# Sums of products (Strassen-Winograd form) in a Hymba-style encoder: three PSUM banks for five, and wider dead products at the start

## The chip, the cores and the metric

The kernel runs on one core of one Trainium2 chip. The metric is the device time of one execution in microseconds (us), here the median of the runs shown. PE is TensorE (matmul), DVE VectorE, ACT ScalarE, POOL GpSimd, SP SyncE, which issues the DMAs.

## The reference

Two token streams (512 and 256 tokens, 768 in all, width 1024) go through two layers. Each layer is an attention block of three mixers with a residual, and then a SwiGLU FFN with a residual; only the FFN is touched by most of the change:

```
h = rms_norm(x, norm_ffn[l])
gate, up = split(h @ w_gate_up[l], 2)          # 1024 -> 2 x 2816
x = x + (silu(gate) * up) @ w_down[l]          # 2816 -> 1024
```

All is float32. The matmuls take operands split in a high and a low part (`fp32r`), so each product is three matmuls: high x high, high x low, low x high.

## The kernel before

**Plan.** The kernel does not issue instructions directly. Each piece of work is an operation of a `Plan` with a cost, a priority, the buffers it reads and writes, and one or more engines that may do it. The planner (`schedule`, `latest`, `emit`) lists all operations of the whole kernel in order, with modelled times, up to 16 times over, gives each buffer a place, picks the best of the orders, and only then issues each engine's instructions in it. So a change of cost or dependence anywhere may move work elsewhere. PSUM has 8 banks of 512 columns; buffers of kind `ANY` take any of them, kind `M` the last. A product that adds to a bank comes after every read of that bank that stands before it in the program.

**Start.** x is loaded in eight pieces, with the first weights between them. While they come, PE runs `WARM` dead matmuls on a tile of ones (line 543). Then the projections of the first head group run on the first 256 tokens, as weight splits (lines 592 and 593) and input splits (lines 650 to 653) come ready; line 834 (ACT, squares) is the first step behind them, and lines 877 and 885 the split and the transposes at the end of that chain.

**FFN, gate and up.** 22 blocks f of 128 gate and up columns; the first two in the plain way, the other 20 with seven products in place of eight (`PRODUCTS`, line 1140). The tokens are two halves of 384 and the input depth two halves of 512. The weights of a block are four 512-wide pieces, from which `sums` (line 1119) makes S1 to S4 in four DVE additions (line 1131), and then splits all seven in high (ACT, line 1134) and low (DVE or POOL, line 1135). `product` (line 1143) is one of the seven: 4 pieces of depth, 3 matmuls of 384 columns each, into one bank.

Before, the seven use five banks: X takes A11 A, then adds S2 T2, then adds S3 T3; Y takes A12 B, Z takes S4 D, W takes A22 T4, V takes S1 T1. After each product into X, ACT copies the bank (line 1193) to one of the four parts of an SBUF buffer `sg`; the other banks are added to parts by DVE (line 1198), five additions in all. Then all four parts are multiplied by the row of norm factors (line 1205), gate goes through Silu (line 1160), is multiplied by up (line 1161) and is written to a DRAM buffer, `spill`.

**FFN, down.** The 22 blocks are taken in five stretches: 6 plain, 4 with sums, 4 plain, 4 with sums, 4 plain. A stretch with sums (`seven`, line 1241) takes two pairs of blocks as depth (n = 2, so 6 matmuls for a product) and goes over 4 pairs of output columns c and c + 4. Its products are read from the banks by DVE, which adds them into x (line 1259): nine additions for a pair.

Of the kernel before, what the change touches and what calls it, by code (L numbers as in the profile page):

```python
# [8 lines left out]
F32 = mybir.dt.float32  # L9
F32R = mybir.dt.float32r  # L10
AF = mybir.ActivationFunctionType
OP = mybir.AluOpType
# [3 lines left out]
D = 1024  # L16
# [6 lines left out]
HALF = 384  # L23
# [4 lines left out]
FIRST_F = 2  # L28
EPS = 1e-6
NEG = -1e30  # L30
WARM = 26
NSTK = 1
RW = 127
GROUPS = ((0, 1), (2, 3, 4), (5, 6, 7))
# [337 lines left out]
def trunk(ctx: ExitStack, tc: tile.TileContext, t):  # L372
    nc = tc.nc
    ACT, DVE, POOL, PE, SP = nc.scalar, nc.vector, nc.gpsimd, nc.tensor, nc.sync
    P = Plan()
# [13 lines left out]
    X = sb("x", [KC, TOK])  # L389
    identr = sb("identr", [128], F32R)  # L390
    ident = identr.bitcast(F32)
    ones = sb("ones", [128], F32R)
# [23 lines left out]
    for i in range(2):  # L416
        at = [(16 + 5 * i + j) * TOK for j in range(5)]
# [71 lines left out]
    def act(n, fn, r=(), w=(), prio=0.0, sbuf=True, extra=0, after=()):  # L489
        return P.op("ACT", a_cost(n, sbuf, extra), fn, r, w, prio, after, lat=0.05)  # L490

    def dve(n, fn, r=(), w=(), prio=0.0, fast=False, lock=False, ptr=False):
        return P.op("DVE", v_cost(n, fast, ptr), fn, r, w, prio, lat=0.05, lock=lock)
# [42 lines left out]
    P.op("DVE", 0.2, lambda: DVE.memset(ones.bitcast(F32), 1.0), w=["ones"], prio=-100)  # L536
    act(128, lambda: ACT.copy(identr, tmp[0]), r=[tmp], w=["identr", "ident"], prio=-15)

    warm = P.buf("M")

    def warmup():
        for _ in range(WARM):
            PE.matmul(warm[0][:, 0:128], ones, ones, start=True, stop=True)

    P.op("PE", 4.0, warmup, r=["ones"], w=[warm], prio=-100)

    def load_gains(l, m, prio):
        b = P.buf("QKG")
# [570 lines left out]
    def sums(srcs, width, prio, after):  # L1119

        q = {m: P.buf("RX") for m in ("A11", "A22", "S1", "A12", "S3", "S2", "S4")}
        b = {m: P.buf("WG") for m in ("A11", "A12", "S2", "S4", "S3", "A22", "S1")}
        hi = lambda m: b[m][0][:, :width]
        lo = lambda m: b[m][0][:, 512:512 + width]
        raw = lambda m: q[m][0][:, :width]
        for m, i in (("A11", 0), ("S1", 2), ("A22", 3), ("A12", 1)):
            out = (lambda m=m: raw(m).rearrange("p (c d) -> p c d", c=srcs[i].shape[1])) if len(srcs[i].shape) == 3 else lambda m=m: raw(m)
            dma(128 * 4 * width, lambda out=out, i=i: SP.dma_start(out=out(), in_=srcs[i]), w=[q[m]], prio=prio, after=after)
        for out, x, y, op in (("S3", "S1", "A11", OP.subtract), ("S1", "S1", "A22", OP.add), ("S2", "A11", "S1", OP.subtract),
                              ("S4", "A12", "S2", OP.add)):  # L1130
            ew(width, lambda E, out=out, x=x, y=y, op=op: E.tensor_tensor(raw(out), raw(x), raw(y), op=op), r=[q[x], q[y]],  # L1131
               w=[q[out]], prio=prio, on="wadd")
        for m in b:
            act(width, lambda m=m: ACT.copy(hi(m), raw(m)), r=[q[m]], w=[(b[m], 0)], prio=prio)  # L1134
            ew(width, lambda E, m=m: E.tensor_tensor(lo(m), raw(m), hi(m).bitcast(F32), op=OP.subtract),  # L1135
               r=[q[m], (b[m], 0)], w=[(b[m], 1)], prio=prio, on="slo")
        return b


    PRODUCTS = (("A11", "A", "X"), ("A12", "B", "Y"), ("S2", "T2", "X"), ("S4", "D", "Z"), ("S3", "T3", "X"), ("A22", "T4", "W"),  # L1140
                ("S1", "T1", "V"))

    def product(wb, ub, bank, n, prio, tok, first, last, open_=True, at=0):
        for kk in range(0, n, 2):
# [10 lines left out]
    def emit_ffn(l, base, ends, row, U):  # L1155
# [24 lines left out]
        for f in range(FIRST_F, FC):  # L1180
            pr = base + f
            wb = sums([t["w_gu"][l, f, i] for i in range(4)], 512, pr - 1.5, ends)
            bank = {}
            sg = P.buf("SG")
            for x, (wn, un, bn) in enumerate(PRODUCTS):
                if bn not in bank:
                    bank[bn] = P.buf("ANY")
                pp = pr + 0.1 * x
                product(wb[wn], [U[k][un] for k in range(4)], bank[bn], 4, pp, utok, un == "A" or bn != "X", True)
                pw = pp - 0.05  # L1190
                if bn == "X":
                    i = ("A", "T2", "T3").index(un)
                    act(HALF, lambda sg=sg, i=i, b=bank["X"]: ACT.copy(sg[i], b[0][:, :HALF]), r=[bank["X"]], w=[(sg, i)],  # L1193
                        prio=pw, sbuf=False)
                else:
                    for dst, src, op in {"Y": ((0, 0, OP.add),), "Z": ((1, 1, OP.add),), "W": ((3, 2, OP.add),),
                                         "V": ((1, 1, OP.add), (2, 2, OP.add))}[bn]:
                        dve(HALF, lambda sg=sg, dst=dst, src=src, op=op, b=bank[bn]: DVE.tensor_tensor(  # L1198
                            sg[dst], sg[src], b[0][:, :HALF], op=op), r=[bank[bn], (sg, src)], w=[(sg, dst)], prio=pw)

            for h, (g, u) in enumerate(((0, 3), (1, 2))):
                rt = [(row, p) for p in ((2, 0) if h == 0 else (0, 1))]
                rv = lambda h=h: row[0][:, h * HALF:(h + 1) * HALF]
                for z, on in ((g, "rg"), (u, "ru")):
                    ew(HALF, lambda E, z=z, sg=sg, rv=rv: E.tensor_tensor(sg[z], sg[z], rv(), op=OP.mult), r=rt, w=[(sg, z)],
                       prio=pr + 0.5, on=on)
                lastsilu = gated(f, sg, g, u, h, pr + 0.5)
# [33 lines left out]
        def seven(f0, n, pd):  # L1241

            us = [operands(f0 + i, f0 + n + i, pd - 15 + 2 * i) for i in range(n)]
            parts = lambda b: [(b, 0), (b, 1)]
            m = 4 // n if n < 4 else 1
            for c2 in range(0, 4, m):
                src = lambda c, f: t["w_down"][l, c:c + m, :, f * 128:(f + n) * 128].rearrange("c p d -> p c d")
                wb = sums([src(c2, f0), src(c2, f0 + n), src(c2 + 4, f0), src(c2 + 4, f0 + n)], m * n * 128, pd + 2 * c2 - 3.5, ())
                for z in range(m):
                    c, bank = c2 + z, {}  # L1250
                    for x, (wn, un, bn) in enumerate(PRODUCTS):
                        if bn not in bank:
                            bank[bn] = P.buf("ANY")
                        pp = pd + 2 * c + 0.2 * x
                        product(wb[wn], [u[un] for u in us], bank[bn], n, pp, parts, un == "A" or bn != "X", True, at=z * n * 128)
                        for cc, h in {"A": ((c, 0),), "B": ((c, 0),), "T2": ((c, 1),), "D": ((c, 1),), "T3": ((c + 4, 0), (c + 4, 1)),
                                      "T4": ((c + 4, 0),), "T1": ((c, 1), (c + 4, 1))}[un]:
                            xv = lambda cc=cc, h=h: X[:, cc, h * HALF:(h + 1) * HALF]
                            dve(HALF, lambda xv=xv, b=bank[bn]: DVE.tensor_tensor(xv(), xv(), b[0][:, :HALF], op=OP.add), r=[bank[bn]],  # L1259
                                w=[("x", p, cc // 2) for p in ((2, 0) if h == 0 else (0, 1))], prio=pp - 2)  # L1260

        for ci, (n, sums_) in enumerate(DCH):
            pd = base + 100 + 20 * ci
# [169 lines left out]
```

## Time and profile before

| | |
|---|---|
| time, median of 3 runs | 1723.81 us (1723.49 to 1727.6) |
| the profiled execution: its time | 1724.8 us |
| its span, first to last instruction | 1722.9 us |
| PE, PE weight loads | 98%, 96% busy |
| DVE, ACT, POOL | 81%, 55%, 36% busy |

The profile is one execution. An engine's busy share is an average over stages; PE's busy time is modelled at its ends, since matmuls overlap. A line such as `PE ps L617 <- ACT y L1193: 2.6, 3, 1.4` says that PE stood 2.6 us in all, 3 times, 1.4 us the longest, until ACT's instruction of line 1193 had finished.

### The profile page before, as it was taken

The page shows a single profiled execution, that of the slowest core. Times are in us where ns is not written, and L with a number is a line of the kernel's source. Part 1 is how long each engine was busy: PE and PEld are TensorE (multiplying, and loading weights), DVE is VectorE, ACT ScalarE, POOL GpSimd, SP SyncE. Part 2 cuts the span into 40 slices and gives each one's busy share as a digit, 9 for nine tenths or more (in the row PEclk, how much of TensorE's full clock was granted, in tenths as well). Part 3 has the DMA queues.
Part 4 walks back from the last instruction along what each step waited for, and adds up shares of the span by engine and source line. Part 5 has one row for each costly group of instructions (what it writes and reads, how often), then busy time and mean ns, then how long its engine had stood idle before and what let it go on. Part 6 is the DMA issues. An engine that isn't in the chain of part 4 may idle for free. (4 is left out here: it accounts for less than half of the span.)

```text
span 1722.9 us, 31174 instructions
## 1 busy us (share of the span) xinstructions
PE 1687.9 (98%) x11434; PEld 1660.9 (96%) x11434; DVE 1390.4 (81%) x2609; ACT 943.7 (55%) x2194; POOL 614.1 (36%) x620
## 2 busy tenths in 40 slices
PE   9999999899999999999999999998999999999999
PEld 8999999899999999999999999997999999999999
DVE  7778678699988887778868886877999887868693
ACT  7877577574444444424458865866744444434230
POOL 1655254223433333224126633632242333323130
PEclk9999999999999999999999999999999999999999
DMA  6221111102433333524322201101133333334233
GB/s 182 73 69 39 38 47 40 50 31 89 132 99 103 97 103 112 155 57 130 97 64 65 77 25 38 57 26 50 47 126 101 102 101 102 108 116 138 80 111 99
DMA packets 102890, 145.31 MB, mean 84 GB/s; under 512 B 29008, under 2 KB 66896, under 8 KB 102736
## 3 DMA queue, kind: packets, MB, share of 16 engines
q1 hardware_dynamic: 102736, 143.31, 27.7%
q8 instruction: 90, 1.47, 0.4%
q14 instruction: 64, 0.52, 0.1%
HBM read 122.82 MB, written 20.45 MB: 83 GB/s over the span
## 5 line engine op out<-in xcount | busy, mean ns | idle before, releaser
L617 PE MATMUL ps<-u,w 128*128 128x384 f32 (+1 forms) x1588 | 526.8, 332 | 8.4 <-ACT y L1193 4.2
L618 PE MATMUL ps<-u,w 128*128 128x384 f32 (+1 forms) x1588 | 525.8, 331 | 0.0
L619 PE MATMUL ps<-u,w 128*128 128x384 f32 (+1 forms) x1588 | 525.6, 331 | 0.0
L617 PEld LDWEIGHTS ps<-u,w 128*128 128x128 f32 x1588 | 298.5, 188 | 11.9 <-ACT y L1193 6.4
L618 PEld LDWEIGHTS ps<-u,w 128*128 128x128 f32 x1588 | 298.5, 188 | 0.3 <-POOL u L1218 0.3
L619 PEld LDWEIGHTS ps<-u,w 128*128 128x128 f32 x1588 | 298.5, 188 | 0.0
L617 PE MATMUL ps<-w,u 128*128 128x256 f32 x768 | 227.1, 296 | 0.4 <-DVE ppa L835 0.2
L618 PE MATMUL ps<-w,u 128*128 128x256 f32 x768 | 219.4, 286 | 0.9 <-DVE w L593 0.7
L619 PE MATMUL ps<-w,u 128*128 128x256 f32 x768 | 219.2, 285 | 0.0
L618 PEld LDWEIGHTS ps<-w,u 128*128 128x128 f32 x768 | 148.6, 193 | 3.0 <-DVE w L593 2.0
L617 PEld LDWEIGHTS ps<-w,u 128*128 128x128 f32 x768 | 148.2, 193 | 2.1 <-DVE ppa L835 0.4
L592 ACT CAST w<-raw 128x1024 fp32r<-128x1024 f32 (+2 forms) x86 | 78.1, 908 | 129.6 <-PE ps L618 90.6
L619 PEld LDWEIGHTS ps<-w,u 128*128 128x128 f32 x768 | 148.4, 193 | 0.2
L1198 DVE TENSOR_TENSOR y<-y,ps 128x384 f32<-128x384 f32 x160 | 86.0, 548 | 59.9 <-PE ps L619 33.1
L617 PE MATMUL ps<-yt,w 128*128 128x256 f32 x392 | 114.1, 291 | 2.1 <-DVE x L1104 1.6
L1020 DVE TENSOR_TENSOR u<-ps,u 128x512 fp32r<-128x512 f32 (+1 forms) x160 | 98.2, 625 | 20.0 <-ACT u L1019 19.1
L618 PE MATMUL ps<-yt,w 128*128 128x256 f32 x392 | 111.8, 285 | 1.1 <-POOL yt L1090 0.8
L619 PE MATMUL ps<-yt,w 128*128 128x256 f32 x392 | 111.2, 284 | 0.0
L1034 PE MATMUL ps<-u 128*128 128x256 f32 (+1 forms) x592 | 102.9, 291 | 6.0 <-DVE u L1020 4.6
L619 PE MATMUL ps<-u,yt 128*128 128x384 f32 x292 | 97.5, 334 | 0.0
L617 PE MATMUL ps<-u,yt 128*128 128x384 f32 x292 | 97.5, 334 | 0.0
L618 PE MATMUL ps<-u,yt 128*128 128x384 f32 x292 | 97.5, 334 | 0.0
(284 smaller groups left out, 3972.3 us busy)
## 6 DMA issues: line engine op xcount, KB each, us to landing
spill<-y SPq DMA_DIRECT2D x86, 192.0 KB, 2.4
raw<-in_w_gu SPq DMA_DIRECT2D x63, 256.0 KB, 2.8
raw<-in_w_in SPq DMA_DIRECT2D x30, 512.0 KB, 3.7
p<-in_w_gu SPq DMA_DIRECT2D x44, 256.0 KB, 2.8
ppa<-in_w_gu SPq DMA_DIRECT2D x39, 256.0 KB, 2.9
raw<-in_w_out SPq DMA_DIRECT2D x16, 512.0 KB, 3.6
tbm<-in_w_gu SPq DMA_DIRECT2D x30, 256.0 KB, 2.9
raw<-in_w_down SPq DMA_DIRECT2D x16, 384.0 KB, 3.4
```

Of the source, the lines that this page charges most:

```text
L592: act(n, lambda raw=raw, hs=hs: ACT.copy(self.flat(0)[:, hs], raw[0][:, :n]), r=[raw], w=[(b, 0) + z], prio=pr)
L617: PE.matmul(out, a[0], b[0], start=start, stop=False, skip_group_check=on)
L618: PE.matmul(out, a[0], b[1], start=False, stop=False, skip_group_check=on)
L619: PE.matmul(out, a[1], b[0], start=False, stop=stop, skip_group_check=on)
L1020: dve(n, lambda n=n, pt=pt, ps_=ps_: DVE.tensor_tensor(ps_[1][:, :n], pt[0][:, :n], ps_[0][:, :n].bitcast(F32), op=OP.subtract), r=[pt, (p ...
L1034: PE.matmul(po[0][:, o:o + wd], v, ps_[i][:, z * wd:(z + 1) * wd], start=first and z == 0 and i == 0, stop=end and (last or more), **({} i ...
L1198: dve(HALF, lambda sg=sg, dst=dst, src=src, op=op, b=bank[bn]: DVE.tensor_tensor(sg[dst], sg[src], b[0][:, :HALF], op=op), r=[bank[bn], (s ...
```

## The change

Three things are changed together.

- The dead matmuls at the start are 15 of 512 columns in place of 26 of 128. They read a buffer `wide` of kind `YT`, which DVE fills with ones first.
- The seven products run in another order and in three banks. X takes A11 A, adds S2 T2, adds S3 T3, adds A22 T4; Y takes A12 B; V takes S1 T1 and adds S4 D. `OPENS` names the products that begin a bank. X is read after each of its four products and V after both of its two.
- What stands behind the products: in gate and up, ACT copies the bank after A, T2 and T1; DVE adds it after B, T3 and D; after T4, DVE multiplies the bank with the row and writes the fourth part, so the row product of that part is no more. In the down stretches each product is added into x once, seven additions for nine.

```diff
-WARM = 26
+WARM = 15
...
-    warm = P.buf("M")
+    warm, wide = P.buf("M"), P.buf("YT")
 
     def warmup():
         for _ in range(WARM):
-            PE.matmul(warm[0][:, 0:128], ones, ones, start=True, stop=True)
+            PE.matmul(warm[0], ones, wide[0], start=True, stop=True)
 
-    P.op("PE", 4.0, warmup, r=["ones"], w=[warm], prio=-100)
+    P.op("DVE", 0.35, lambda: DVE.memset(wide[0].bitcast(F32), 1.0), w=[wide], prio=-100)
+    P.op("PE", 4.0, warmup, r=["ones", wide], w=[warm], prio=-100)
...
-        b = {m: P.buf("WG") for m in ("A11", "A12", "S2", "S4", "S3", "A22", "S1")}
+        b = {m: P.buf("WG") for m in ("A11", "A12", "S2", "S1", "S3", "S4", "A22")}
...
-    PRODUCTS = (("A11", "A", "X"), ("A12", "B", "Y"), ("S2", "T2", "X"), ("S4", "D", "Z"), ("S3", "T3", "X"), ("A22", "T4", "W"),
-                ("S1", "T1", "V"))
+    PRODUCTS = (("A11", "A", "X"), ("A12", "B", "Y"), ("S2", "T2", "X"), ("S1", "T1", "V"), ("S3", "T3", "X"), ("S4", "D", "V"),
+                ("A22", "T4", "X"))
+    OPENS = ("A", "B", "T1")
...
-                product(wb[wn], [U[k][un] for k in range(4)], bank[bn], 4, pp, utok, un == "A" or bn != "X", True)
-                pw = pp - 0.05
-                if bn == "X":
-                    i = ("A", "T2", "T3").index(un)
-                    act(HALF, lambda sg=sg, i=i, b=bank["X"]: ACT.copy(sg[i], b[0][:, :HALF]), r=[bank["X"]], w=[(sg, i)],
-                        prio=pw, sbuf=False)
+                product(wb[wn], [U[k][un] for k in range(4)], bank[bn], 4, pp, utok, un in OPENS, True)
+                pw, at, z = pp - 0.05, lambda b=bank[bn]: b[0][:, :HALF], {"A": 0, "B": 0, "T2": 1, "T1": 2, "T3": 2, "D": 1, "T4": 3}[un]
+                if un in ("A", "T2", "T1"):
+                    act(HALF, lambda sg=sg, z=z, at=at: ACT.copy(sg[z], at()), r=[bank[bn]], w=[(sg, z)], prio=pw, sbuf=False)
+                elif un == "T4":
+                    dve(HALF, lambda sg=sg, z=z, at=at: DVE.tensor_tensor(sg[z], at(), row[0][:, :HALF], op=OP.mult),
+                        r=[bank[bn], (row, 2), (row, 0)], w=[(sg, z)], prio=pw)
                 else:
-                    for dst, src, op in {"Y": ((0, 0, OP.add),), "Z": ((1, 1, OP.add),), "W": ((3, 2, OP.add),),
-                                         "V": ((1, 1, OP.add), (2, 2, OP.add))}[bn]:
-                        dve(HALF, lambda sg=sg, dst=dst, src=src, op=op, b=bank[bn]: DVE.tensor_tensor(
-                            sg[dst], sg[src], b[0][:, :HALF], op=op), r=[bank[bn], (sg, src)], w=[(sg, dst)], prio=pw)
+                    dve(HALF, lambda sg=sg, z=z, at=at: DVE.tensor_tensor(sg[z], sg[z], at(), op=OP.add), r=[bank[bn]], w=[(sg, z)],
+                        prio=pw)
...
-                for z, on in ((g, "rg"), (u, "ru")):
+                for z, on in ((g, "rg"), (u, "ru"))[:2 if h else 1]:
...
-                        for cc, h in {"A": ((c, 0),), "B": ((c, 0),), "T2": ((c, 1),), "D": ((c, 1),), "T3": ((c + 4, 0), (c + 4, 1)),
-                                      "T4": ((c + 4, 0),), "T1": ((c, 1), (c + 4, 1))}[un]:
+                        cc, h = {"A": (c, 0), "B": (c, 0), "T2": (c, 1), "T1": (c + 4, 1), "T3": (c + 4, 1), "D": (c, 1), "T4": (c + 4, 0)}[un]
```

## Rows read from the trace of the kernel before

**Rows 1.** The page's head: span and busy time of each engine

```profile
span 1722.9 us, 31174 instructions
...
PE 1687.9 (98%) x11434; PEld 1660.9 (96%) x11434; DVE 1390.4 (81%) x2609; ACT 943.7 (55%) x2194; POOL 614.1 (36%) x620
```

**Rows 2.** Windows: stretch, its length, engines' busy time (instructions), clock, DMA, GB/s

```profile
10.00:395.00 385.00, 375.00 (x2933) 364.67 (x2934) 310.64 (x704) 285.14 (x753) 164.55 (x200) 1.00 0.20 60
...
440.00:650.00 210.00, 209.48 (x1207) 208.84 (x1206) 179.20 (x265) 92.44 (x175) 74.77 (x58) 1.00 0.35 105
...
860.00:1245.00 385.00, 373.85 (x2961) 362.13 (x2959) 303.63 (x682) 274.88 (x724) 155.37 (x190) 1.00 0.17 49
...
1290.00:1490.00 200.00, 200.00 (x1155) 199.81 (x1154) 169.59 (x253) 87.86 (x167) 67.78 (x55) 1.00 0.33 100
```

**Rows 3.** Timeline of PE, 0 to 34 us: start, duration, instruction, idle before

```profile
1.09 5.81 PE L543 MATMUL ps<-ones 128*128 128x128 f32 x26 [1.09 <-DVE ones L536]
6.73 0.58 PE L617 MATMUL ps<-w,u 128*128 128x256 f32 x1
...
17.11 0.56 PE L617 MATMUL ps<-w,u 128*128 128x256 f32 x1
...
20.25 0.41 PE L619 MATMUL ps<-w,u 128*128 128x256 f32 x1
20.46 0.39 PE L617 MATMUL ps<-w,u 128*128 128x256 f32 x1
...
20.80 0.28 PE L619 MATMUL ps<-w,u 128*128 128x256 f32 x1
20.92 0.28 PE L617 MATMUL ps<-w,u 128*128 128x256 f32 x1
...
33.66 0.54 PE L885 MATMUL ps<-identr,u 128*128 128x128 f32 x4 [1.34 <-DVE u L877]
```

**Rows 4.** Timeline of DVE and ACT, 0 to 23 us

```profile
0.87 0.17 DVE L536 MEMSET ones<- 128x128 f32 x1
...
6.06 0.62 ACT L592 CAST w<-raw 128x512 fp32r<-128x512 f32 x1 [1.79 <-DMA raw<-in_w_in]
...
22.55 0.49 ACT L834 ACTIVATE ppa<-ps 128x384 f32<-128x384 f32 x1 [2.00 <-PE ps L619]
```

**Rows 5.** Whom PE waited for, 395 to 860, then 1245 to 1723

```profile
PE ps L617 <- ACT y L1193: 2.6, 3, 1.4
PE ps L617 <- DVE x L1259: 1.9, 2, 1.6
...
PE ps L617 <- DVE x L1259: 2.3, 2, 1.6
PE ps L617 <- ACT y L1193: 1.6, 1, 1.6
```

**Rows 6.** Single lines, whole run: count, duration ns (min/median/max), first and last start

```profile
L1198 DVE TENSOR_TENSOR y<-y,ps x160: 539/547/555, 404.6 to 1542.4; 128x384 f32<-128x384 f32 x160
...
L1205 DVE TENSOR_TENSOR y<-y,row x102: 543/557/1685, 406.5 to 1544.2; 128x384 f32<-128x384 f32 x102
...
L1259 DVE TENSOR_TENSOR x<-x,ps x144: 539/548/555, 738.1 to 1685.2; 128x384 f32<-128x384 f32 x144
```

**Rows 7.** Timeline of ACT and PE at the entry to gate and up, layer 0

```profile
406.71 0.62 ACT L1134 CAST yt<-ppa 128x512 fp32r<-128x512 f32 x1 [1.42 <-DVE ppa L1131]
...
408.27 0.47 ACT L1193 COPY y<-ps 128x384 f32<-128x384 f32 x1
...
408.80 0.44 PE L617 MATMUL ps<-u,w 128*128 128x384 f32 x1 [1.38 <-ACT y L1193]
```

**Rows 8.** Timeline of DVE and PE, last down stretch with sums, layer 0

```profile
815.15 1.50 DVE L1135 TENSOR_TENSOR w<-raw,w 128x512 fp32r<-128x512 f32 x1
816.57 1.94 DVE L1259 TENSOR_TENSOR x<-x,ps 128x384 f32<-128x384 f32 x4
...
818.19 0.41 PE L617 MATMUL ps<-u,w 128*128 128x384 f32 x1 [1.62 <-DVE x L1259]
```

More of the change, by code (lines that the diff above doesn't have):

```diff
@@ L1254, in seven @@
                         pp = pd + 2 * c + 0.2 * x
-                        product(wb[wn], [u[un] for u in us], bank[bn], n, pp, parts, un == "A" or bn != "X", True, at=z * n * 128)
-                        for cc, h in {"A": ((c, 0),), "B": ((c, 0),), "T2": ((c, 1),), "D": ((c, 1),), "T3": ((c + 4, 0), (c + 4, 1)),
-                                      "T4": ((c + 4, 0),), "T1": ((c, 1), (c + 4, 1))}[un]:
-                            xv = lambda cc=cc, h=h: X[:, cc, h * HALF:(h + 1) * HALF]
-                            dve(HALF, lambda xv=xv, b=bank[bn]: DVE.tensor_tensor(xv(), xv(), b[0][:, :HALF], op=OP.add), r=[bank[bn]],
-                                w=[("x", p, cc // 2) for p in ((2, 0) if h == 0 else (0, 1))], prio=pp - 2)
+                        product(wb[wn], [u[un] for u in us], bank[bn], n, pp, parts, un in OPENS, True, at=z * n * 128)
+                        cc, h = {"A": (c, 0), "B": (c, 0), "T2": (c, 1), "T1": (c + 4, 1), "T3": (c + 4, 1), "D": (c, 1), "T4": (c + 4, 0)}[un]
+                        xv = lambda cc=cc, h=h: X[:, cc, h * HALF:(h + 1) * HALF]
+                        dve(HALF, lambda xv=xv, b=bank[bn]: DVE.tensor_tensor(xv(), xv(), b[0][:, :HALF], op=OP.add), r=[bank[bn]],
+                            w=[("x", p, cc // 2) for p in ((2, 0) if h == 0 else (0, 1))], prio=pp - 2)
         for ci, (n, sums_) in enumerate(DCH):
```

## The prediction

> **What bounds the kernel now.** I read the page first: TensorE (PE) is busy 98% of the span, VectorE (DVE) 81% [rows 1]. Then busy time by stretch [rows 2]. In the two stretches of gate and up products, 440 to 650 us and 1290 to 1490 us, PE is idle 0.5 us and 0.0 us. There 1155 matmuls fill 200 us, 0.173 us each, and DVE is busy 85% of that time: PE is the bound, and everything else is beneath it. In the attention stretches PE is idle 10.0 and 11.2 us of 385. So time can come out of three places only: what PE executes, the gaps in attention, and a few waits around the FFN. The view of who PE waits for names the last ones [rows 5]: ScalarE's (ACT) copies out of PSUM, line 1193, 4 times and 4.2 us in both layers together (2.6 + 1.6), and DVE's additions into x, line 1259, 4 times and 4.2 us (1.9 + 2.3). That is 8.4 us, and it lies at the entry to the gate and up products and around the down products.
>
> PE's timeline from the start shows one thing more [rows 3]. The 26 dead products take 5.81 us; afterwards real products of 256 columns start 0.21 us apart (20.25, 20.46), and from 20.8 us on 0.12 us apart (20.80, 20.92). [...] So the dead products of before did not bring the clock up: it rose only after an unbroken run of real ones from 17.11. (The granted-clock column reads 1.00 for 10 to 395 us [rows 2]; the starts do not bear that out before 20.5, and I go by the starts.)
>
> **The change part by part.**
>
> *Products.* There are seven per pair as before, with 12 matmuls each in gate and up (4 in depth, 3 each) and 6 each in the down sums. PE's work is the same: 0 us. All lie at 0.173 us, whatever the bank.
>
> *Additions.* For each of the 40 (layer, f) pairs, DVE's additions out of PSUM go from 5 to 4, the fourth takes the row product with it, and one row product of four goes. For each of the 16 column pairs of the down sums, additions go from 9 to 7. That is 40 x 0.547 + 40 x 0.557 + 32 x 0.548 = 61.7 us less on DVE at most [rows 6]. It is hidden: in the steady stretches PE waits for nothing, so this costs and brings 0 there. It counts only where DVE is late, in the 8.4 us.
>
> *Banks read between products.* Before, bank X was read twice and then written again in each set of seven (after A and after T2). Now X is read three times and written again, and V once (T1 before D): 4 re-reads for 2. That is 160 for 80 in gate and up and 64 for 32 in the down sums. Each has one other product as cover: 12 x 0.173 = 2.08 us in gate and up, 6 x 0.173 = 1.04 us in the down sums. A read takes 0.55 us, so it may start 1.5 us late in the first and 0.5 us late in the second before PE stands, unless the planner puts another set's product between. In gate and up a copy that came late shows what happens: the copy at 408.27 stood behind casts of weights, the first of which had waited 1.42 us for DVE's sums, and PE stood 1.38 us [rows 7]. In the down sums DVE worked off weight splits (the one at 815.15 took 1.50 us) before its additions at 816.57, and PE stood 1.62 us [rows 8]. Whether that product waited for its own bank to be read or for a free one, the rows do not say; fewer banks helps the second and more re-reads hurts the first. Bounds: all 8.4 us go (-8.4), or they double with the re-reads (+8.4). For the first end speaks that the new order asks for S4, last of the chain of weight sums, sixth instead of fourth, and that DVE has two operations fewer for each f. For the other end, the cover of the down sums is half as long, and there the re-reads also double. I take the two long waits at the entries (1.4 and 1.6 us, 3.0 together) as gone and two new ones of the mean size (8.4 / 8 = 1.0 us) in the down sums: -1.0 us.
>
> *Clock during these waits.* Waits of 1.38 and 1.62 us between products left the granted clock at 1.00 in every stretch [rows 2, 7, 8], so I charge nothing for it. [...]
>
> *Dead products.* Now 15 of 512 columns in place of 26 of 128. The new fill of 512 columns on DVE costs between the 0.17 us that 128 columns took and four times that, 0.68 [rows 4]; so they start at 1.2 to 1.7 us instead of 1.09. At the slow level a product of 512 columns is twice the 0.213: 0.427 us, 15 are 6.4 us and end at 8.1 at the latest; at the fast level twice 0.12, 3.6 us. The first real product started at 6.73, when its weights' cast (6.06 + 0.62) was done. The rise at 20.5 came after an unbroken run of real products, none after the dead ones of 128 columns; wide dead products in a row resemble that run more than they resemble the old ones. So I take the clock as up from about 7 us, which no row shows.
>
> What is that worth? Not half of 13 us, since the first part waits for weight splits anyway. After the products of the first 256 tokens ACT stood 2.00 us for PE (line 834, 22.55) [rows 4]; with the faster clock PE is done before ACT is, and this wait goes. The chain behind it (norms, rotation, split, transposes) then reaches the transposes at 33.66, for which PE stood 1.34 us [rows 3], up to 2.0 us earlier, and PE has its own work done earlier by more than that: from 17.11 to 20.46 it ran 16 products (3.35 / 0.213), which cost 16 x (0.213 - 0.12) = 1.5 us too much, and those before it more. So -2.0 us; bounds: 0, if the splits on DVE are what is late next (or the clock stays down), and +1.2 us if the dead products end at 8.1 instead of 6.9 with the clock still down. The trace of before shows no such block, hence the width.
>
> *The plan.* One planner orders all engines over the whole kernel, so other costs give another order in attention too. How much a different order is worth I bound by the two layers, which do the same there: 10.0 against 11.2 us idle [rows 2], so about 1.2 us for each, 2.4 in all, of either sign: 0 in the sum.
>
> *Sum.* 1724.8 (the profiled execution's own time) - 2.0 - 1.0 = 1721.8. That execution is 1.0 above the median of the runs, so 1720.8 against 1723.81.
>
> **The rivals.** 0.3% is 5.2 us here, about what this kernel's measurement can tell from no change.
>
> *A, as summed:* start gains 2.0, the FFN's waits hardly move. 1720.8, own range 1717 to 1725. Chance 0.54.
>
> *B, the waits go:* fewer banks held and 61.7 us less on DVE clear most of the 8.4 us. In full 1724.8 - 2.0 - 8.4 - 1.0 = 1713.4; from 3.2 us of them on it is faster by over 0.3%. For it: DVE is near full at the entries, where the waits lie. Against it: ACT and the chain of weight sums, not the additions, stood ahead of the late copy [rows 7]. Chance 0.21.
>
> *C, the re-reads stall PE:* this is the one on the other side. The waits double with their number, above all in the down sums with 1.04 us of cover: 1724.8 - 2.0 + 8.4 - 1.0 = 1730.2. It decides from 7.2 us of new waits on (5.2 and the 2.0 of the start). For it: there were already 4 waits on 32 re-reads there. Against it: the planner knows the banks and kept 76 of 80 free in gate and up. Chance 0.13.
>
> *D, the dead products do not raise the clock*, or it falls again while PE waits for splits between 8 and 14 us: the start brings nothing or costs up to 1.2; 1722.8 to 1724.0. Chance 0.10.
>
> [...] Chance 0.02. [...]
>
> **How the numbers follow.** The predicted time is that of A. Faster by over 0.3% (below 1718.6): B's 0.21, and 0.04 of A's lower end, 0.25. Slower (above 1729.0): most of C and E, 0.13. The same: 0.62. The range leaves out the ends of B and of C: 1716 to 1728.
>
> **What would show it.** Right: products of 256 columns 0.12 us apart from about 7 us on; no wait of 2.0 us at line 834; PE idle 0 to 1 us in both steady stretches; PE's waits for the copies and for the additions into x of 6 to 9 us in sum; DVE's busy time near 1330 us. Wrong: starts 0.21 apart until 20 us (D); waits for the reads out of PSUM in the down sums above 12 us (C), or under 4 us in all (B); PE more than 2 us further apart in an attention stretch than before, which would put the difference on the plan and not on the products.

## The result and the profile after

The changed kernel takes 1733.39 us (median of 4 runs, 1733.01 to 1734.83), the kernel before 1724.61 beside it: ratio 1.0051 [1.0039, 1.0064]. It is slower by 0.5%, some 8.8 us, and outside the forecast range.

The page's head of the changed kernel, which answers to [rows 1]. In its line PEclk each digit is a fortieth of the span:

```profile
span 1731.7 us, 30968 instructions
...
PE 1692.8 (98%) x11423; PEld 1666.3 (96%) x11423; DVE 1333.0 (77%) x2491; ACT 943.4 (54%) x2194; POOL 628.9 (36%) x627
...
PEclk8999999999999999999999999999999999999999
```

DVE lost 57.4 us of work, nearly what was forecast, and the span grew by 8.8. The single lines of the changed kernel that answer to [rows 6] show where the work went:

```profile
L1199 DVE TENSOR_TENSOR y<-y,ps x100: 535/553/555, 409.6 to 1542.5; 128x384 f32<-128x384 f32 x100
...
L1199 DVE TENSOR_TENSOR sq<-sq,ps x20: 541/547/554, 411.7 to 1525.8; 128x384 f32<-128x384 f32 x20
...
L1259 DVE TENSOR_TENSOR x<-x,ps x112: 537/553/556, 739.7 to 1686.4; 128x384 f32<-128x384 f32 x112
```

[rows 6] show 160 sums of line 1198; the same line has 40 more on another buffer in the kernel before:

```profile
L1198 DVE TENSOR_TENSOR sq<-sq,ps x40: 540/544/555, 414.7 to 1526.8; 128x384 f32<-128x384 f32 x40
```

So there are 120 sums for 200 and 112 additions into x for 144, each as long as before within 1.5%. Of the 80 sums that are gone, 40 became the product with the row (line 1196).

Windows of the changed kernel (columns as in [rows 2]), first the stretches shown there, then three short ones and one around a long wait, and under them the last short one in the kernel before:

```profile
10.00:395.00 385.00, 376.01 (x2929) 365.30 (x2930) 313.13 (x708) 284.13 (x748) 152.85 (x192) 0.98 0.20 59
...
440.00:650.00 210.00, 208.62 (x1202) 208.13 (x1201) 160.40 (x228) 90.66 (x172) 86.20 (x65) 1.00 0.33 105
...
860.00:1245.00 385.00, 376.09 (x2976) 366.77 (x2975) 307.54 (x690) 274.91 (x724) 157.70 (x191) 0.99 0.17 50
...
1297.00:1490.00 193.00, 193.00 (x1114) 193.00 (x1113) 142.65 (x207) 84.75 (x161) 81.26 (x62) 1.00 0.33 100
...
12.00:20.00 8.00, 7.24 (x35) 6.80 (x35) 8.00 (x21) 7.80 (x21) 0.00 (x0) 0.57 1.04 345
...
1290.00:1297.00 7.00, 5.17 (x21) 5.17 (x22) 5.61 (x9) 0.92 (x2) 1.21 (x1) 0.76 0.01 2
1685.00:1696.00 11.00, 6.71 (x33) 6.10 (x33) 3.56 (x4) 2.89 (x3) 1.42 (x2) 0.69 0.56 163
...
400.00:450.00 50.00, 46.75 (x268) 46.38 (x269) 44.66 (x71) 26.44 (x52) 18.27 (x14) 1.00 0.41 132
```

```profile
1685.00:1696.00 11.00, 11.00 (x93) 10.83 (x92) 5.10 (x8) 2.09 (x2) 0.27 (x1) 1.00 0.34 109
```

The steady stretch of layer 1 is as full as before: 193.00 of 193 us. Attention has less idle time, not more (9.0 and 8.9 us of 385, against 10.0 and 11.2). What is new are the short stretches with a clock under 1.00. In the one from 1685 us on PE ran 33 products where the kernel before ran 93.

Whom PE waited for in the changed kernel, 395 to 860, then 1245 to 1731 (answers to [rows 5]):

```profile
PE ps L618 <- ACT y L1194: 3.3, 2, 3.1
PE ps L618 <- DVE x L1259: 2.1, 3, 1.2
PE ps L618 <- DVE y L1199: 1.4, 1, 1.4
...
PE ps L618 <- ACT w L593: 3.8, 1, 3.8
PE ps L618 <- DVE sq L1199: 1.9, 1, 1.9
...
PE ps L618 <- DVE x L1259: 1.0, 2, 0.5
```

(Of the lines named here those from 546 on count one higher than before; line 1259 is the same.) The additions into x cost PE 3.1 us, less than the 4.2 before. None is over 1.2 us, for the 1.62 of [rows 8]. The largest wait is of a kind that [rows 5] do not have at all: for ACT's cast of a weight.

The timeline of the changed kernel at the three places, layer 0's entry to gate and up (answers to [rows 7]), layer 1's entry, and layer 1's last down stretch:

```profile
402.06 0.51 ACT L718 CAST u<-p 128x384 fp32r<-128x384 f32 x1 [1.31 <-DVE p L754]
402.48 0.47 ACT L1194 COPY y<-ps 128x384 f32<-128x384 f32 x1
403.01 0.45 PE L618 MATMUL ps<-u,w 128*128 128x384 f32 x1 [3.07 <-ACT y L1194]
...
1291.83 0.44 PE L618 MATMUL ps<-u,w 128*128 128x384 f32 x1 [1.89 <-DVE sq L1199]
...
1682.25 0.93 ACT L1218 CAST u<-raw 128x384 fp32r<-128x384 f32 x2 [8.34 <-PE ps L620]
1684.43 1.99 POOL L1219 TENSOR_TENSOR u<-raw,u 128x384 fp32r<-128x384 f32 x2 [9.79 <-issue]
1685.47 8.47 SPq L590 DMA_DIRECT2D raw<-in_w_down  x4
1689.11 1.04 ACT L593 CAST w<-raw 128x1024 fp32r<-128x1024 f32 x1 [5.93 <-DMA raw<-in_w_down]
1690.20 0.58 PE L618 MATMUL ps<-u,w 128*128 128x256 f32 x1 [3.83 <-ACT w L593]
1691.46 0.58 PE L620 MATMUL ps<-u,w 128*128 128x256 f32 x1 [0.46 <-DVE w L594]
...
1692.06 0.41 PE L619 MATMUL ps<-u,w 128*128 128x256 f32 x1
1692.27 0.41 PE L620 MATMUL ps<-u,w 128*128 128x256 f32 x1
```

The transfer of the same weights in the kernel before, from SP's queue:

```profile
1669.95 14.73 SPq L589 DMA_DIRECT2D raw<-in_w_down  x4
```

Read the last stretch from its end. PE stood 3.83 us at 1690.20 for ACT's cast of the first weights (1689.11), ACT 5.93 us for their DMA, and SP issued that DMA at 1685.47. Before, it was issued at 1669.95, 14 us ahead of its stretch. In between lies a buffer: the DMA goes into `raw`, which also holds the last blocks of `spill` until ACT (1682.25, after 8.34 us of waiting for PE) and POOL (1684.43) have split them. Then products of 256 columns start 0.21 us apart (1692.06, 1692.27), as at the lower of the two levels in [rows 3], where they have 0.12 at the higher one. The granted clock is 0.50 from 1691 to 1693 us; in the whole window from 1685 to 1696 it is 0.69.

The start of the changed kernel, PE first, then ACT (answers to [rows 3, 4]):

```profile
1.62 5.66 PE L543 MATMUL ps<-yt,ones 128*128 128x512 f32 x15 [1.62 <-DVE yt L545]
7.12 0.28 PE L618 MATMUL ps<-w,u 128*128 128x256 f32 x1
7.24 0.28 PE L619 MATMUL ps<-w,u 128*128 128x256 f32 x1
...
10.61 0.38 PE L618 MATMUL ps<-w,u 128*128 128x256 f32 x1 [0.61 <-ACT w L593]
...
13.59 0.58 PE L619 MATMUL ps<-w,u 128*128 128x256 f32 x1 [0.76 <-DVE w L594]
...
18.85 0.41 PE L620 MATMUL ps<-w,u 128*128 128x256 f32 x1
19.06 0.41 PE L618 MATMUL ps<-w,u 128*128 128x256 f32 x1
...
32.86 0.60 PE L886 MATMUL ps<-identr,u 128*128 128x128 f32 x4 [1.82 <-DVE u L878]
...
22.00 0.49 ACT L835 ACTIVATE ppa<-ps 128x384 f32<-128x384 f32 x1 [1.59 <-PE ps L620]
```

The wide dead products did raise the clock: starts 0.12 us apart from 7.12. It fell again at 12.7 us (0.21 apart at 18.85; 0.57 granted from 12 to 20 us) after PE had waited for splits by 0.3 to 0.6 us at a time, the longest at 10.61. The first transposes came at 32.86 for 33.66, and ACT's wait at what was line 834 is 1.59 for 2.00.

**Where the 8.8 us lie.** I cut the trace by PE's products of 384 columns (attention has hardly any): a layer's part goes from the first of them to the first product of the last stretch behind them, so that a wait ahead of that stretch counts in it. The last stretch of layer 0 is thus in what is called attention of layer 1 here. Up to the first product of 384 columns: 350.9 us against 351.2. Layer 0's part 482.0 for 479.6, attention of layer 1 373.9 for 375.9, layer 1's part 483.5 for 477.4, the last stretch 37.3 for 34.6 us. So layer 1's FFN with its last stretch is 8.7 longer, layer 0's 2.4, and attention gives some 2 back. In layer 1's FFN PE's idle time grew by 4.0 (3.88 to 7.89). The records also name the falls of the clock: after 20 us none before, and after the change at 33, 327, 1180, 1190, 1293 and 1689 us. The products inside these took about 8 us more than at the full level (an estimate from the starts of this run: 256 columns take 0.213 us inside them and 0.119 outside, so 0.094 more, and other widths in proportion); the two of layer 1's FFN 1.6 and 2.0. That is 4.0 + 3.6 of the 8.7.

### The profile page after: what moved, and what is told of

It reads as the page before. It is cut to its first block, busy times and chain, and to the rows that moved or that the text cites. A ratio compares the mean times of both kernels' runs of the same rounds, so it can differ in the third digit from the quotient of the medians.

```text
span 1731.7 us, 30968 instructions
## 1 busy us (share of the span) xinstructions
PE 1692.8 (98%) x11423; PEld 1666.3 (96%) x11423; DVE 1333.0 (77%) x2491; ACT 943.4 (54%) x2194; POOL 628.9 (36%) x627
## 4 chain that ended last, share of the span: by engine, by line
PE 81%; DVE 10%; ACT 3%; issue 3%; DMA 2%; SPq 0%; POOL 0%; DVEq 0%; ACTq 0%; POOLq 0%
PE ps L618 23%; PE ps L619 23%; PE ps L620 23%; PE ps L1035 4%; PE ps L954 3%; PE ps L1013 3%; PE ps L886 1%; DVE w L594 1%; DVE w L1136 1%; DVE u L721 1%; PE ps L1062 1%; DVE u L724 1%; DVE u L1238 1%; DMA ppa<-spill 1%; DVE p L780 0%
## 5 line engine op out<-in xcount | busy, mean ns | idle before, releaser
L1035 PE MATMUL ps<-u 128*128 128x256 f32 (+1 forms) x592 | 102.8, 292 | 3.0 <-DVE y L1050 2.2
L1199 DVE TENSOR_TENSOR y<-y,ps 128x384 f32<-128x384 f32 x100 | 55.0, 550 | 63.0 <-PE ps L620 40.3
L954 PE MATMUL ps<-u 128*128 128x256 f32 (+1 forms) x384 | 97.6, 353 | 3.3 <-ACT p L962 2.3
L618 PE MATMUL ps<-u,yt 128*128 128x384 f32 x292 | 98.1, 336 | 0.0
L620 PE MATMUL ps<-u,yt 128*128 128x384 f32 x292 | 98.0, 336 | 0.0
## 6 DMA issues: line engine op xcount, KB each, us to landing
raw<-in_w_in SPq DMA_DIRECT2D x30, 512.0 KB, 3.7
raw<-in_w_out SPq DMA_DIRECT2D x16, 512.0 KB, 3.6
```

What stands on the lines that cost most here:

```text
L618: PE.matmul(out, a[0], b[0], start=start, stop=False, skip_group_check=on)
L620: PE.matmul(out, a[1], b[0], start=False, stop=stop, skip_group_check=on)
L954: PE.matmul(S[0][:, :nk], q, kk[:, k0:k0 + nk], start=i == 0, stop=i == 1)
L1035: PE.matmul(po[0][:, o:o + wd], v, ps_[i][:, z * wd:(z + 1) * wd], start=first and z == 0 and i == 0, stop=end and (last or more), **({} i ...
L1199: dve(HALF, lambda sg=sg, z=z, at=at: DVE.tensor_tensor(sg[z], sg[z], at(), op=OP.add), r=[bank[bn]], w=[(sg, z)], prio=pw)
```

## The experiments

Two theories. **Form:** seven products in three banks cost time in themselves, as rival C said, by re-reads that PE waits for. **Order (O):** the form is free or nearly so, and the planner, given other costs, has picked an order with other waits, which the clock then makes dearer. The changed kernel's edits are taken apart first, then the order is changed with the work held fixed. In the expectations theory P and theory O stand for the order, R and F for the form; theories 1 and 2 ask whether the loss hangs on the products or on the new start. Orders are counted from 0, so that order 14 is the fifteenth.

"FFN" in the table is both layers' parts and the last stretch, cut as above from one profiled execution; "falls" are the starts of stretches at the lower clock after 22 us. Each ratio is to the kernel before as run beside that kernel, where its median was 1724.6 to 1725.5 us.

| kernel | median us | ratio to before | FFN us | falls |
|---|---|---|---|---|
| before | 1724.61 | 1 | 991.9 | none |
| after | 1733.39 | 1.0051 [1.0039, 1.0064] | 1003.0 | 33, 327, 1180, 1190, 1293, 1689 |
| e1 dead products only | 1726.42 | 1.0004 [0.9996, 1.0013] | 992.4 | 328 |
| e2 products only | 1735.37 | 1.0054 [1.0041, 1.0066] | 1006.2 | 34, 324, 403, 1181, 1191, 1294, 1693 |
| e3 gate and up only | 1725.36 | 1.0003 [0.9994, 1.0012] | 992.6 | 43, 1258 |
| e4 down only | 1733.87 | 1.0044 [1.0032, 1.0056] | 999.4 | 830 |
| e5 after, order 14 | 1728.42 | 1.0026 [1.0016, 1.0036] | 993.3 | 331, 406 |
| e6 after, order 1 | 1732.68 | 1.005 [1.0037, 1.0062] | 993.9 | 874, 1198 |
| e13 after, order 11 | 1734.57 | 1.0054 [1.0039, 1.0069] | 993.7 | 326, 408 |
| e14 after, order 2 | 1734.13 | 1.0055 [1.0037, 1.0073] | 998.5 | 919, 1260 |
| e7 before, order 5 | 1727.39 | 1.0014 [1.0005, 1.0023] | 990.0 | 326, 917 |
| e15 before, order 4 | 1719.28 | 0.9968 [0.9956, 0.998] | 986.7 | none |
| e16 before, order 2 | 1739.74 | 1.0083 [1.0068, 1.0098] | 1005.3 | 832, 1122, 1695 |
| e8 after, filled wait | 1730.43 | 1.0035 [1.0022, 1.0047] | 1001.9 | 33, 402, 1177 |
| e9 after, own places | 1739.72 | 1.008 [1.0066, 1.0094] | 997.6 | 327, 402, 876, 924 |
| e10 before, own places | 1728.28 | 1.0019 [1.0011, 1.0028] | 996.7 | 1180 |
| e11 gate and up, own places | 1738.75 | 1.0078 [1.0065, 1.0091] | 1007.7 | 400, 806, 1666 |
| e12 dead products, clock kept | 1722.66 | 0.9989 [0.998, 0.9998] | 992.0 | 326 |
| e17 before, order 4, clock kept | 1718.47 | 0.9955 [0.9942, 0.9967] | 987.8 | 321 |
| e18 after, order 14, clock kept | 1728.9 | 1.0018 [1.0009, 1.0027] | 995.3 | 327, 405 |

**Parts of the change.** e1 has the first two hunks of the diff alone, e2 all the others. e3 has the new products in gate and up alone, e4 in the down stretches alone, both with the old dead products:

```diff
+    OLD = (("A11", "A", "X"), ..., ("S1", "T1", "V"))      # five banks, old order
-                    for x, (wn, un, bn) in enumerate(PRODUCTS):   # in seven()
+                    for x, (wn, un, bn) in enumerate(OLD):        # e3; e4 the same in gate and up
```

> Only the dead products change (15 of 512 columns for 26 of 128); the seven products stay in five banks. Theory 1 (the loss lies in the products: PE waits for reads between them, and for the last weights): 1723 to 1726 us, the start shorter by 0 to 1 us, no wait of 3 us in the last stretch. Theory 2 (the loss hangs on the new start: once the clock has come up early it falls again at waits that it stood before): 1728 to 1733 us, with falls of the clock in attention and in the FFN.

> Only the products change (order, three banks, the reads behind them); the old dead products stay. Theory 1: 1731 to 1735 us, with the 3.8 us wait for the last stretch's weights. Theory 2: 1723 to 1728 us, the clock up at about 20 us and not falling afterwards.

> The new products in gate and up alone, the down stretches in five banks as before, the old dead products. If the re-reads in gate and up and the operands T1 that they need earlier cost the time: 1726 to 1729 us, with waits of 3 us at the entry of layer 0. If the loss is the place of buffers in the last stretch: 1723 to 1726 us, and no long wait there.

> The new products in the down stretches alone, gate and up in five banks, the old dead products. If the loss is in the down stretches (re-reads with 1.04 us of cover, or the last stretch's weights late): 1728 to 1733 us. If it is in gate and up: 1723 to 1726 us.

The dead products bring nothing (1.0004). The gate and up form costs nothing in the order that it got (1.0003), though it has 40 of the 56 sets of seven and 160 of the 224 re-reads. The down form alone is 1.0044, almost the whole loss. The largest of its waits of PE, 395 to 860 us in e4, is not one of rival C:

```profile
PE ps L617 <- ACT w L592: 3.3, 1, 3.3
PE ps L617 <- ACT y L1196: 2.4, 1, 2.4
PE ps L617 <- DVE x L1261: 2.3, 3, 1.0
```

Additions into x cost 2.3 us there (1.9 before, [rows 5]); the new one is a cast of weights, 3.3 us, as in the changed kernel but in the other layer. That speaks for the order, but e3 and e4 have one order each, so they can't tell the form from the order that came with it. In layer 1 e4 has no wait for late weights and is still 4 to 5 us longer than the kernel before, 2.6 of it idle time of PE.

**Other orders of the same work.** The planner keeps the order with the shortest modelled span. Here it keeps another:

```diff
-            if best is None or span < best[0]:
+            if i == 14:          # e5; e6: 1, e13: 11, e14: 2; in the kernel before e7: 5, e15: 4, e16: 2
```

> The changed kernel, instruction for instruction the same work, but in the fifteenth of the planner's sixteen orders in place of the ninth, which the planner chose (its own model gives 1697.8 us for this order, 1695.9 for the chosen one, and 1696.0 for the order of the kernel before; the model's gap ahead of the last stretch is 2.3 us here and 5.5 us there). Theory P (the loss is the order: where the long waits lie, and the clock that falls behind them): 1726 to 1731 us, gate and up, down and last stretch of layer 1 together within 3 us of the kernel before. Theory R (reading banks between products costs PE time in any order): 1732 to 1736 us, and those stretches at least 6 us longer than before.

> The changed kernel in the second of the planner's orders (model 1699.1 us; no gap ahead of either last stretch, but 22.3 us and 19.2 us of gaps in attention for 18.4 and 16.1 in the chosen order). Theory P: 1727 to 1733 us, the FFN of layer 1 within 2 us of the kernel before, attention longer than in the changed kernel by 4 to 8 us in both layers together. Theory R: 1735 to 1740 us, the FFN no shorter than in the changed kernel.

> The kernel before, the same work, in the sixth of its planner's orders (model 1701.3 us for 1696.0 of the chosen one). Theory P: 1727 to 1734 us, that is, as slow as the changed kernel without any of the change in it. Theory R: 1723 to 1727 us, since the five banks are kept.

> The changed kernel in the twelfth of the planner's orders (model 1701.9 us; 2.1 us of gap ahead of the last stretch of layer 0, 0.6 in layer 1). Theory O (order): the FFN parts of both layers together 990 to 996 us (991.6 in the kernel before, 1002.8 in the changed one), the time 1730 to 1736 with longer attention. Theory F (the three-bank form costs): FFN parts 998 us or more.

> The changed kernel in the third order (model 1702.2 us, 3.0 us ahead of the last stretch of layer 1). Theory O: FFN parts 992 to 998 us, the time 1729 to 1736. Theory F: FFN parts 998 us or more.

> The kernel before in the fifth of its planner's orders (model 1701.2 us, 2.2 and 1.5 us ahead of the last stretches). Theory O: FFN parts 990 to 996 us, as the three-bank orders; the time 1727 to 1733. Theory F: FFN parts 993 us or less.

> The kernel before in the third order (model 1707.8 us; gaps of 6.1 and 4.2 us ahead of the last stretches). Theory O: the five-bank kernel with such gaps is as slow as the changed one: FFN parts 998 to 1006 us, the clock falling ahead of a last stretch, the time 1733 to 1740. Theory F: FFN parts under 995 us, the time under 1731.

The kernel before, with the same operations in other orders (an order also moves up to 14 of them between DVE and POOL), takes 1719.3 to 1739.7 us: 20 us, more than twice what the change cost. The changed one takes 1728.4 to 1734.6. The planner's own figures (a model) had the chosen orders at 1696.0 before and 1695.9 after, equal; for the kernel before it put 1701.2 on order 4, measured as the fastest, and 1707.8 on order 2, the slowest. What PE waited for shows how: 395 to 860 us in e5 and in e15, and 395 to 1740 us in e16 (its first and third row):

```profile
PE ps L618 <- ACT y L1194: 4.5, 1, 4.5
```

```profile
PE ps L617 <- ACT y L1193: 1.9, 2, 1.1
PE ps L617 <- DVE x L1259: 0.7, 1, 0.7
```

```profile
PE ps L617 <- ACT w L592: 9.2, 2, 5.6
...
PE ps L617 <- DVE x L1259: 3.9, 4, 1.6
```

e5 has the changed kernel's re-reads and no wait for an addition into x in layer 0 at all, but one of 4.5 us for a copy out of a bank at the entry to gate and up. e16 has five banks and stands for weights, 9.2 us in two waits, one ahead of each layer's last stretch, with the clock falling in both (832 and 1695). So late weights come with an order and do not need the three-bank form. e6 and e13 have an FFN of 994 us, but lose ahead of it, in attention (379.3 us in layer 1 for 375.9, and about 355 for 351 up to the first product of 384 columns).

Not all of this came out as the theory of order had it. e5, e6, e13 and e16 did in their times and their FFN, e7 lies where the two ranges meet. e14's FFN (998.5 us, forecast 992 to 998) and e15's (986.7, forecast 990 to 996) fell on the side of theory F, and e15 is 8 us faster than the theory of order put it: five banks can do better than was thought.

What settles part of it is a sum over the FFN. Take off PE's waits of more than 0.15 us, each with the late product behind it, and what products at the lower clock took beyond the usual 0.1733 us (384 columns) and 0.1193 us (256). Then 982.0 us are left in the changed kernel and 982.0 in the kernel before, 980.7 to 982.5 in the other orders of both, and 984.6 in e14. So the FFN's 11.2 us are waits (17.0 us for 9.6) and the lower clock (3.7 for 0), and there the three-bank form can cost time only through waits and the clock. PE's waits behind reads of banks are 9.7, 7.2, 6.1, 6.2 and 7.3 us in the five orders of the changed kernel (after, e5, e6, e13, e14), 8.4, 5.7, 4.8 and 6.2 in the four of the kernel before (before, e7, e15, e16): 7.3 and 6.3 on average.

**The clock by itself.** e8 is the changed kernel with 20 dead products ahead of the last stretch, where PE stands anyway:

```diff
-                    def mm(j=j, o=o, pc=pcs[cp], acc=acc):
+                    def mm(j=j, o=o, pc=pcs[cp], acc=acc, dead=(l, p, cp, j) == (1, 0, 0, 0)):
+                        for _ in range(20 if dead else 0):
+                            PE.matmul(acc[0][:, :HALF], ones, ab[0][0][0][:, :HALF], start=True, stop=True)
```

> The changed kernel with 20 dead matmuls of 384 columns (3.5 us of PE) issued in the wait of 3.8 us ahead of the last stretch; they write a bank that the next product begins anew. If the clock that falls in this wait costs by itself: the last stretch at full clock from its start and the time 1.5 to 2.5 us less than the changed kernel, 1731 to 1732. If only the late weights count: no change or up to 0.5 us more, 1733 to 1735.

Its windows over that place:

```profile
1685.00:1690.00 5.00, 3.77 (x24) 3.24 (x24) 2.32 (x2) 2.09 (x2) 0.00 (x0) 1.00 0.47 170
1690.00:1700.00 10.00, 10.00 (x86) 10.00 (x85) 4.47 (x6) 2.10 (x2) 0.00 (x0) 1.00 0.51 166
```

The weights come no earlier, but the clock stays at the higher level: from its first real product on the last stretch takes 35.8 us for 37.6 (34.9 in the kernel before), and layer 1's FFN with it 519.0 us for 520.8. The time is 1730.43, 3.0 less, though the intervals of the two ratios overlap. The order is otherwise that of the changed kernel, and yet the falls at 327, 1190 and 1293 are absent and one at 402 is new. A fall does not belong to a place alone, and what of the 3.0 us is more than the last stretch's 1.8 may lie there.

**The late weights by themselves.** e9 keeps the last blocks' loads out of the two places that the weights behind them need (`RXL`), so that the weights need not wait for them; e10 does so in the kernel before, e11 in e3:

```diff
+    P.storage("RXL", [(a,) for a in r0[4:] + cut(pt_, "p", 4, 512) + cut(tbm, "tb", 2, 512)])
...
-                q = P.buf("RX")
+                q = P.buf("RXL" if kind == "UL" else "RX")
```

> The changed kernel, where the loads of the last stretch of blocks may no longer take the two places that the weights behind them need (nine places left for those loads; the model's best order gives 1697.8 us, no gap ahead of the last stretch). If late weights for lack of a place made the wait of 3.8 us: that wait under 1 us, gate and up, down and last stretch of layer 1 512 to 515 us for 520.8, the time 1726 to 1730. If the new products delay that stretch anyhow: the wait stays above 2 us and the time above 1731.

> The same places in the kernel before, five banks (model 1692.7 us, 3.3 less than before, without a gap over 2 us). If the order decides: 1720 to 1723 us, faster than before. If the model's differences of 3 us don't reach the chip: 1724 to 1728.

> Three banks in gate and up, five in the down stretches, the old dead products and the same places (model 1694.5 us). If reading between products costs nothing in gate and up: within 3 us of the run with these places in the kernel before, 1721 to 1726. If it costs: 1728 or more.

In e9 the mechanism is as read: no wait for a weight's cast, no fall behind it, and layer 1's FFN with the last stretch 513.6 us for 520.8 (512.0 before). But the time is worse, 1739.72: attention of layer 1 takes 382.6 us for 373.9. e10 and e11 also run slower than their like without the edit, e11 by 13 us, with a wait of 5.3 us for an addition into x in a five-bank down stretch:

```profile
PE ps L618 <- DVE x L1262: 9.8, 3, 5.3
```

By its expectation e11 speaks for a cost of the form, but its 9.8 us of waits for additions into x lie in the five-bank part. An edit of a few loads moves every stage, so each of the three is another order too. The 7.2 us less in layer 1's FFN of e9 fit the late weights as a cost there (the wait and fall at 1292 are gone too), but the edit is no repair of the kernel.

**The start.** e12 is e1 with three more dead products of 512 columns ahead of each later piece of depth in the first projection, which fill PE's gaps there; e17 is e15 with all of that and the wide dead products, e18 is e5 with the three:

```diff
+                        for _ in range(3 if (l, g, p, j) == (0, 0, 0, 0) and kk else 0):
+                            PE.matmul(pb[6], ones, pc[0].flat(0)[:, :512], start=True, stop=True)
```

> The kernel before with the new dead products, and three more of 512 columns before each of three later parts of the first products, where PE waits for weight splits (they write a bank that nothing reads). If the start lost its gain because the clock fell while PE waited: the clock stays up from 7 to 20 us, the wait for PE at the squares (2.0 us) goes, the first transposes come 1.5 to 2.0 us earlier than 33.66, and the time is 1722.5 to 1724. If DVE's splits bind the start whatever the clock: the transposes within 0.5 us of 33.66, the time 1724 to 1727.

> The kernel before in the planner's fifth order, with the wide dead products and the three more ahead of later parts of the first products. If order and start add up (-5.9 and -2.2 us against the kernel before): 1716 to 1718 us. If the clock in the start only shifts a wait of this order: 1718.5 to 1720.

> The changed kernel in the planner's fifteenth order (1728.4 us) with the three more dead products in the start. If the start adds up here too: 1725.5 to 1727 us, level with the kernel before within 0.15%. If the three banks cost time in this order: the FFN parts above 996 us; if not, 992 to 995 as in the run without the start.

A window of e1, then window and two rows of e12:

```profile
12.00:20.00 8.00, 7.23 (x33) 6.59 (x34) 8.00 (x21) 7.78 (x21) 0.00 (x0) 0.61 1.03 343
```

```profile
12.00:20.00 8.00, 7.36 (x53) 6.66 (x54) 8.00 (x21) 7.72 (x20) 0.00 (x0) 1.00 1.06 351
...
20.49 0.47 ACT L837 ACTIVATE ppa<-ps 128x384 f32<-128x384 f32 x1
...
30.51 0.53 PE L888 MATMUL ps<-identr,u 128*128 128x128 f32 x4 [0.38 <-DVE u L880]
```

With the clock held, ACT's wait is gone (20.49, none) and the transposes come at 30.51, 3.15 us earlier than in [rows 3]; the time falls by 2.2 us, to 0.9989 [0.998, 0.9998]. That is what the prediction wanted of the start, by other means. The clock fell between 12 and 17 us in all eight profiled executions with wide dead products alone (0.57 granted from 12 to 20 us in the changed kernel, 0.61 in e1), and in none of the three with the others added (1.00 in e12; e17, e18). It does not add up with a good order: e17 is 0.8 us under e15, with intervals that overlap, though its transposes come at 31.38; e18 (1.0018) and e5 (1.0026) are not apart either. e17, five banks in order 4, is the fastest of all, 1718.47.

## Why the prediction was wrong

**The step that failed** is "The plan": a different order was bounded at 2.4 us, by the idle time of two attention stretches that do the same work, and went into the sum as 0. That bound looked where the order had been good in both layers. Orders of one and the same kernel measured 20 us apart, between the extremes (e15 and e16) by 18.6 us in the FFN, where [rows 5] had shown only 8.4 us of waits because this one order was good there. What the new order did is above all the cast of late weights: 3.83 and 0.46 us at 1690, not in the sum at all. The sign set for the plan, an attention stretch over 2 us further apart, looked in the wrong stage: attention got shorter.

**"Clock during these waits", charged at nothing**, failed with it. In the kernel before, waits of 1.38 and 1.62 us had left the clock alone. The windows of [rows 2] do not reach those two waits, but the mean clock of the whole run does (its record begins at 20.7 us):

```profile
core 0: 1722.9 us, clock 1.000
```

In the changed kernel falls stand beside a wait of 1.89 us (1291.83) and one of 3.83 us, and 3.6 us in layer 1's FFN went on them, about 8 in the whole run. The length of a wait alone does not decide it: the wait of 3.07 us at 403.01 in the same run left the clock at 1.00 (window from 400 to 450 us). E, which stands in the chances with 0.02, was a fall of the clock over the products of one block f of gate and up in each layer. No run shows that: no fall in the table lies between 440 and 650 us or between 1297 and 1490, and layer 1's steady stretch, with four re-reads in every set of seven, ran at 1.00, 193.00 of 193 us busy. What the changed kernel showed in its place are falls beside the two waits; at 1690 PE waited for a transfer, ACT 5.93 us for the DMA and PE 3.83 behind it, with 0.69 granted from 1685 to 1696 us.

**Start, -2.0:** the clock came up as taken, then fell from 12.7 to 19.5 us (0.50 granted there), the second half of rival D. e1 measures no gain, e12 shows that the fall was what took it.

**Waits, -1.0:** behind the reads of banks 8.4 us became 9.7 (copies and additions into x 6.4, inside the forecast 6 to 9; sums at line 1199, 3.3, new). So +1.3. The copy at 402.48 stood behind a cast of tokens (402.06) that waited for DVE's work on the norms (line 754); the forecast that a long wait at this entry would go was wrong, it grew from 1.38 to 3.07. In gate and up alone the waits behind reads grew from 4.2 to 6.6 us.

The measured time of the profiled execution, 1733.66, is 11.9 us over the forecast 1721.8. By place: up to the first product of 384 columns -0.3 us where the start should have brought -2.0; in the FFN +11.2 where -1.0 was forecast; in attention of layer 1 -2.0 where 0 was. Of the FFN's 11.2, PE's waits with the late products behind them are 7.4 (as idle time, late weights are 4.3 of it and reads of banks 1.3) and the lower clock 3.7.

**What was right:** PE's work is the same; the saving on DVE (57.4 us of 61.7) is hidden; PE is idle 0.0 us in one steady stretch and 1.4 in the other, a single wait for a sum (line 1199), a little over the 0 to 1 forecast. In the down sums PE's waits for additions did not grow (3.1 us for 4.2). So rival C was nearest in time (1730.2), but by luck: of its 8.4 us of new waits behind reads 1.3 came.

**What stays open** is whether the form, in the down sums above all, brings longer waits of its own. No run with it is under 1728.4 us, five-bank ones go down to 1718.5; the shortest FFN is 993.3 us with it and 986.7 without. Five orders of the changed kernel average 1732.6, four of the one before 1727.8 with a spread of 20: the runs do not tell 5 us from nothing. That waits and the clock make the FFN's difference is shown by the sum over the FFN. That an order alone brings such waits is shown by e5 against the changed kernel and by e15 against e16, and late weights with five banks by e16. That the clock costs time by itself is shown in the last stretch by e8 and in the start by e12. How much of the 8.8 us the form has a part in, by the order that it leads the planner to, is not shown.

## What to carry to other kernels

Where one planner orders a whole kernel, small differences of its modelled span need not hold: here spans within 6 us of each other (1695.9 to 1702.2) did not come out in their order on the chip. A small change can then be worth less than the lottery of orders behind it: run several orders of both versions before judging either, and keep the fastest. Before a short last stretch look for the buffers that its weights wait for; a load that had to wait for the stage before it cost its wait here (3.83 us) and then the clock (2.0). Work that an engine off the path is spared (57.4 us of DVE's here) brought nothing: look for a wait that it would end in the trace before counting it.

## What was not expected of the hardware

- After 15 dead products of 512 columns in 5.66 us the clock was up by 7.12 us (products 0.12 us apart); after 26 of 128 columns in 5.81 us it was not (0.21 apart until 20.5 us) [rows 3].
- It fell at 12.7 us behind gaps of PE of only 0.3 to 0.6 us each, and later beside single waits of 1.89 and 3.83 us. Beside one of 3.07 us (403.01) in the same execution it did not, nor beside those of 1.38 and 1.62 us in the kernel before.
- Two executions of the same order (changed kernel and e8, alike but for the 20 dead products at its end) show falls at different places: 327, 1190 and 1293 in one, 402 in the other.
